# Layer 1's attention written out as a pipeline over three engines, its filler dealt out block by block, one PSUM bank each for values and filler

## The chip, the core and the metric

The kernel runs on one core of a Trainium2 chip. The time is that of one launch on the device, in microseconds (us). Three executions of the kernel before took 1471.29, 1473.4 and 1473.78 us; their median, 1473.4 us, is the time before.

Five engines work in parallel, each through its own list of instructions in a fixed order: PE (matrix products and transposes), DVE and ACT (element by element, reductions, exponentials), POOL (element by element, slower) and SP (starts the transfers). An instruction that has to wait for another engine holds up all that stands behind it on its own engine.

## The reference, cut to what matters

Two layers over 512 latent and 256 context tokens of width 1024. The change is in the attention of layer 1, the last layer, where only the latent tokens are still needed:

```
z = h @ w_in                                     # q (8 heads of 64), k, v (2 heads), u and g of a gated MLP
s = einsum('bkgqd,bkmd->bkgqm', qblk, k)         # per head and 128 queries: 128 x 768 scores
p = softmax(s, axis=-1)
o = einsum('bkgqm,bkmd->bkgqd', p, v)
x = x + ga1 * (concat([attn, gm]) @ w_out)       # gm: the gated MLP's output, ready before the attention
x = x + ga2 * sqrelu_mlp(modulate(rmsnorm(x)))   # 1024 -> 4096 -> 1024
```

Each product is of 32-bit floats. The kernel splits an operand into a high and a low part (two or three products for one); the split is a cast on ACT (`hi`) and a subtraction on DVE or POOL (`lo`).

## The kernel before, in words

Weights come in blocks of 128x1024. SP loads a block into one of two `raw` buffers, ACT casts it to `hi` (L221), POOL or DVE makes `lo` (L222, called a conversion below); five such pairs can be live.

Layer 1's attention has 32 tiles: four pairs of heads j, two blocks of 256 queries, two heads hh, two halves qt of 128 queries. For a tile (`attn_tile`, L1029) PE makes 128x768 scores into one of two `pa` buffers (four matmuls, L217), DVE takes the negated maximum (L1041), ACT the exponential with its sum into a buffer `w` (L1046; tag `w` has three buffers, and L712 takes the same tag for each piece of the q projection, until L733 has read it). In `second`, PE turns the tile by six transposes into two buffers `pt` (L1057), ACT casts them (L1059) and DVE subtracts (L1060). In `third`, once for two tiles (a group), PE makes the values by twelve matmuls into a `pb` buffer (L1080), ACT copies half of it (`pv`, L1087), DVE adds (`mix`, L1088) and, for the second head, multiplies by the softmax factor that PE has transposed next to it (L1084, L1090), and POOL splits the result into Q (L1093, L1094).

Beside that runs the filler: the half of the output projection that works on `gm`, eight outputs m of four k blocks, three matmuls of 128x512 per block (`gm_out`, `proj4`). Each output goes to a `pb` buffer and is added to the residual X by `gate`: in this place ACT scales it (L988) and POOL adds it (L989). The other half, on Q, comes after the attention, by the same `proj4`, with `gate` on DVE (L991). Just ahead of the attention, the last pieces of the q projection are still going through DVE and POOL (L712 to L727), then split (L732, L733) and turned (L745, L746) into Q.

The order on each engine comes from a planner: the program is traced in one sequence, a counter `fl.vt` of estimated time says when deferred steps (`second`, `third`, conversions) and fillers are traced, and a scheduler then puts the instructions of each engine into an order by that sequence and its own cost estimates. In a region under `tc.manual_schedule` an engine's order is that of the trace. `pb` buffers, two in all, were handed out as they came free.

Of the kernel before, what the change touches and what calls it, by code (L numbers as in the profile page):

```python
# [8 lines left out]
F32 = mybir.dt.float32  # L9
# [3 lines left out]
ALU = mybir.AluOpType  # L13
# [19 lines left out]
LATE = (None, None)  # L33


PAR = {"KF": 1, "XO": 1, "MS": 3, "KB": 6, "S0": 200.0, "S2": 1.0, "BK": 1, "CS": 0, "S1": 2400.0, "NS": 2, "CX": 0,
# [135 lines left out]
def trunk(ctx: ExitStack, tc: tile.TileContext, xT, pk1, pk2, rope, wsT, w_mod, w_tok, w_u, w_out, w_ff1, w_ff2, outT):  # L172
# [12 lines left out]
    def nm(s):  # L185
        seq[0] += 1
        return f"{s}_{seq[0]}"
# [7 lines left out]
    def tsm(shape, dt=F32):  # L195
        return tmp.tile(shape, dt, tag="s", name=nm("s"), bufs=3)
# [10 lines left out]
    def pa():  # L207
        return psum.tile([128, 1024], F32, tag="a", name=nm("pa"), bufs=2)

    def pb(shape=(128, 512)):  # L210
        return psum.tile(list(shape), F32, tag="b", name=nm("pb"), bufs=2)

    def pt(shape=(128, 512)):
        return psum.tile(list(shape), F32, tag="t", name=nm("pt"), bufs=2)
# [1 line left out]
    def mm(out, a, b, start, stop, n):  # L216
        pe.matmul(out, a, b, start=start, stop=stop)  # L217
        fl.vt += max(n / 2.4, 113.0) + 3.0

    def split(hi, lo, src, eng=None):  # L220
        act.copy(hi, src)  # L221
        (eng or vec).tensor_tensor(out=lo, in0=src, in1=hi.bitcast(F32), op=ALU.subtract)  # L222
# [5 lines left out]
    ready = []  # L228
    RING = 5

    held = []

    def convert():

# [3 lines left out]
    def pump():  # L238
        while state["live"] < RING and state["pos"] < len(order):
            key = order[state["pos"]]  # L240
            if key == ("ctx",):
                for i in range(4):
                    nc.sync.dma_start(X[i][:, :, SEQ:T], xT[i][:, :, SEQ:T])
                nc.sync.dma_start(k2s[0][:, 128:640], pk2[0][:, 128:640])
                state["pos"] += 1
                continue
            src = dram[key[0]]
            for i in key[1:]:
                src = src[i]
            early = EARLY[state["pos"]] if state["pos"] < len(EARLY) else None  # L250
            if early:
                raw = unit(early, [128, 1024], F32)
            elif key[0] == "mod":

                two = [ring.tile([128, 1024], F32, tag=t, name=nm(t), bufs=RING) for t in ("hi", "lo")]
                for i in range(2):
                    nc.sync.dma_start(two[i], w_mod[0, key[2], key[3] + i])
                ready.append((key, *two))
                state["pos"] += 1
                state["live"] += 1  # L260
                continue
            else:
                raw = ring.tile([128, 1024], F32, tag="raw", name=nm("raw"), bufs=2)
            nc.sync.dma_start(raw, src)
            if key[0] == "mod":
                ready.append((key, raw, None))
                state["pos"] += 1
                continue
            hi = ring.tile([128, 1024], F32R, tag="hi", name=nm("hi"), bufs=RING)
            lo = ring.tile([128, 1024], F32R, tag="lo", name=nm("lo"), bufs=RING)  # L270
            if held is None:
                split(hi, lo, raw, pool_e if "%s%d" % key[:2] in PAR["WP"] else vec)
            else:
                held.append((hi, lo, raw))
            ready.append((key, hi, lo))
            state["pos"] += 1
            state["live"] += 1

    def settle():
        state["live"] -= state["freed"]  # L280
        state["freed"] = 0
        pump()

    def take(*key):
        if not ready:
            settle()
        k, hi, lo = ready.pop([r[0] for r in ready].index(key))
        return hi, lo

# [159 lines left out]
    def region(name):  # L449
        e = PAR["RM"].get(name, "")  # L450
        return tc.manual_schedule(engines={EN[c] for c in e}) if e else nullcontext()
# [235 lines left out]
    def layer(l, h, nxt, K, kv=None, kv0=0):  # L687
# [293 lines left out]
        def gate(i, m, off, n, src):  # L981
            for a, b, cond in ((0, SEQ, 0), (SEQ, T, 1)):
                s, e = max(a, off), min(b, off + n)
                if s < e:
                    xs = xk(m)[:, s:e]
                    if last and i == 2 and done[0] < 8:
                        t = tsm([128, e - s])
                        act.activation(t, src[:, s - off:e - off], AF.Copy, scale=modT[l][:, i * 8 + m, cond:cond + 1])  # L988
                        pool_e.tensor_tensor(out=xs, in0=xs, in1=t, op=ALU.add)  # L989
                        continue  # L990
                    vec.scalar_tensor_tensor(out=xs, in0=src[:, s - off:e - off], scalar=modT[l][:, i * 8 + m, cond:cond + 1], in1=xs, op0=ALU.mult, op1=ALU.add)  # L991

        def proj4(keys, R, i, passes, bank, post=None, gates=None):

            wbs = {}
            for pi, parts in enumerate(passes):
                while gates and not gates[pi]():
                    yield "wait"
                for m in range(8):
                    if m // 2 not in wbs:  # L1000
                        wbs[m // 2] = take(*keys, m // 2)
                    for q, (off, n) in enumerate(parts):
                        if bank == "b":
# [96 lines left out]
        def attention(blks, period):  # L1100
            goal = fl.vt
            for j in range(4):
                for f in turns[0:3 + NP * (1 + j // 2)]:
                    f()
                for blk in blks:
                    st = {}
                    for hh in range(2):
                        for qt in range(2):
                            attn_tile(j, blk, hh, qt, st)
                            fl.tick()  # L1110
                            if last:
                                goal += period
                                fl.fill(goal)
                            else:
                                goal = max(goal, fl.vt) + period
                                fl.step()
                                fl.fill0(goal)

        def gm_out():
            if not GM:  # L1120
                make_gm()
            yield from proj4(("out", l, 0), GM, 2, [dense], "b")
# [36 lines left out]
                    held.append(nr)  # L1159

        fl.fillers = [gm_out(), proj4(("out", l, 1), Q, 2, [[p[0:2]] for p in order2], "b", outpost, gates)]
        with region('att%d' % l):
            if not last:
                fl.fillers = [mods((4, 5)), mixed(fl.fillers[0], mods((6, 7, 8, 9, 10, 11))), fl.fillers[1]]
                attention((2,), PAR["PC"])
            attention((0, 1), PAR["P%d" % l])
        with region('aend%d' % l):
            while done[0] < 8:
                fl.fill(fl.vt + 500.0)
# [233 lines left out]
```

## Time and profile before

| what | value |
|---|---|
| median of three executions | 1473.4 us |
| the profiled execution's own time | 1471.6 us |
| its span | 1469.8 us |
| PE busy | 1437.9 us |
| DVE, ACT, POOL busy | 907.2, 644.2, 379.1 us |
| first scores of layer 1's attention start | 988.35 us |
| first matmul of the output projection on Q starts | 1090.67 us |

All later views are of the profiled execution, in us from the start of its span. A row of the timeline gives start, length, engine, line, operation, output and inputs, and how many equal instructions it merges; in brackets how long the engine had been idle and for whom. On one engine a row's length overlaps the next row's start; from one start to the next is what an instruction takes of its engine.

### The profile page before, as it was taken

To read this page: it belongs to the slowest core of one execution; us is meant where nothing else is said; L and a number is where in the kernel's file an instruction comes from. 1 tells how busy PE (TensorE), PEld (TensorE's weight loads), DVE (VectorE), ACT (ScalarE), POOL (GpSimd) and SP (SyncE) were. 2 spreads that over 40 slices of the span, in tenths; PEclk is the share of its full clock that TensorE was granted. 3 is DMA by queue.
4 is the path that set the end of the run, shared out by engine and by line. 5 is a ranking of instruction groups with operands and counts; after the bars stand their busy time and mean duration, and the time that the engine had idled before them with its cause. 6 is when DMAs were issued, how large, how long until landed. Compare 5 with 4: busy or idle time off the path is not lost.

```text
span 1469.8 us, 21069 instructions
## 1 busy us (share of the span) xinstructions
PE 1437.9 (98%) x8178; PEld 1224.3 (83%) x8178; DVE 907.2 (62%) x1586; ACT 644.2 (44%) x1141; POOL 379.1 (26%) x320
## 2 busy tenths in 40 slices
PE   6999999999999999999999999999999999999998
PEld 3899787988888888888888889997889888888887
DVE  5857867778766564556556547775968554444443
ACT  3552546664545453433325234547855223332221
POOL 0323511222256461323324123277121000000000
PEclk9999999999999999999999999999999999999999
DMA  9322544101233343423343212212002322322331
GB/s 366 116 72 100 188 145 144 59 1 58 90 122 122 118 135 106 136 94 136 106 131 123 88 35 77 96 58 72 16 1 75 120 93 100 100 95 93 100 100 58
DMA packets 50083, 148.71 MB, mean 101 GB/s; under 512 B 5440, under 2 KB 6976, under 8 KB 49984
## 3 DMA queue, kind: packets, MB, share of 16 engines
q1 hardware_dynamic: 49408, 146.72, 29.6%
q8 instruction: 64, 1.05, 0.3%
q10 hardware_dynamic: 576, 0.66, 0.2%
q14 instruction: 35, 0.29, 0.1%
HBM read 145.26 MB, written 2.10 MB: 100 GB/s over the span
## 4 chain that ended last, share of the span: by engine, by line
PE 86%; DVE 7%; ACT 3%; POOL 2%; issue 1%; DMA 1%; SPq 0%; POOLq 0%; ACTq 0%; DVEq 0%
PE pa L217 54%; PE pb L217 23%; PE pt L1057 3%; PE pt L217 2%; PE pb L354 2%; POOL m L298 1%; PE pt L745 1%; DVE lo L222 1%; DMA A<-in_w_mod 1%; POOL lo L222 1%; DVE s L907 0%; ACT hi L221 0%; DVE A L795 0%; ACT w L1046 0%; DVE s L716 0%
## 5 line engine op out<-in xcount | busy, mean ns | idle before, releaser
L217 PE MATMUL pa<-A,hi 128*128 128x512 f32 (+2 forms) x1440 | 429.9, 376 | 0.4 <-ACT A L527 0.2
L221 ACT CAST hi<-raw 128x1024 fp32r<-128x1024 f32 x168 | 176.1, 1049 | 326.9 <-PE pa L217 246.1
L217 PEld LDWEIGHTS pa<-A,hi 128*128 128x128 f32 x1440 | 262.7, 188 | 46.6 <-DVE s L716 0.4
L217 PE MATMUL pa<-A,lo 128*128 128x512 f32 (+2 forms) x832 | 283.8, 347 | 0.0
L222 DVE TENSOR_TENSOR lo<-raw,hi 128x1024 fp32r<-128x1024 f32 x152 | 203.6, 1340 | 122.0 <-ACT hi L221 117.7
L403 POOL TENSOR_TENSOR C<-C,s 128x512 f32<-128x512 f32 x112 | 173.5, 1564 | 296.5 <-ACT s L402 289.8
L217 PE MATMUL pa<-B,hi 128*128 128x512 f32 x750 | 239.0, 391 | 0.0
L217 PEld LDWEIGHTS pa<-A,lo 128*128 128x128 f32 x832 | 156.7, 188 | 21.3
L991 DVE SCALAR_TENSOR_TENSOR X<-pa,modT,X 128x512 f32<-128x512 f32 x168 | 99.8, 614 | 104.6 <-PE pa L217 103.1
L217 PEld LDWEIGHTS pa<-B,hi 128*128 128x128 f32 x750 | 139.9, 188 | 27.2
L217 PE MATMUL pb<-B,hi 128*128 128x512 f32 (+1 forms) x600 | 157.1, 349 | 1.2 <-DVE X L991 1.0
L217 PE MATMUL pa<-B,lo 128*128 128x512 f32 (+1 forms) x450 | 155.2, 354 | 0.0
L217 PE MATMUL pb<-hi,A 128*128 128x256 f32 (+1 forms) x608 | 118.1, 291 | 0.6 <-DVE m L725 0.6
L217 PEld LDWEIGHTS pb<-B,hi 128*128 128x128 f32 x600 | 104.4, 189 | 16.0 <-DVE X L991 2.1
L991 DVE SCALAR_TENSOR_TENSOR X<-pb,modT,X 128x512 f32<-128x512 f32 (+3 forms) x108 | 64.9, 610 | 74.1 <-PE pb L217 74.0
L217 PE MATMUL pb<-B,lo 128*128 128x512 f32 (+1 forms) x300 | 104.1, 347 | 0.0
L217 PEld LDWEIGHTS pb<-hi,A 128*128 128x128 f32 x608 | 96.9, 191 | 2.2 <-PE pb L217 0.8
L217 PEld LDWEIGHTS pa<-B,lo 128*128 128x128 f32 x450 | 84.5, 188 | 14.8
L402 ACT ACTIVATE s<-k,silu 128x512 f32<-128x512 f32 x112 | 77.9, 718 | 35.8 <-DMA k<-in_w_mod 27.8
L217 PE MATMUL pb<-lo,A 128*128 128x256 f32 (+1 forms) x304 | 87.6, 288 | 0.0
L1060 DVE TENSOR_TENSOR A<-pt,A 128x384 fp32r<-128x384 f32 (+1 forms) x144 | 73.6, 536 | 21.1 <-ACT A L1059 19.8
L217 PE MATMUL pb<-A,hi 128*128 128x384 f32 (+2 forms) x288 | 80.4, 360 | 1.1 <-DVE s L833 0.6
(214 smaller groups left out, 2222.6 us busy)
## 6 DMA issues: line engine op xcount, KB each, us to landing
raw<-in_w_ff SPq DMA_DIRECT2D x128, 512.0 KB, 3.5
k<-in_w_mod SPq DMA_DIRECT2D x96, 256.0 KB, 2.8
raw<-in_w_tok SPq DMA_DIRECT2D x16, 512.0 KB, 3.5
raw<-in_w_out SPq DMA_DIRECT2D x16, 512.0 KB, 3.4
lo<-in_w_mod SPq DMA_DIRECT2D x16, 512.0 KB, 4.6
hi<-in_w_mod SPq DMA_DIRECT2D x16, 512.0 KB, 4.0
A<-in_w_mod SPq DMA_DIRECT2D x8, 512.0 KB, 9.8
B<-in_w_mod SPq DMA_DIRECT2D x8, 512.0 KB, 9.6
```

The costliest lines, as they stand in the source:

```text
L217: pe.matmul(out, a, b, start=start, stop=stop)
L221: act.copy(hi, src)
L222: (eng or vec).tensor_tensor(out=lo, in0=src, in1=hi.bitcast(F32), op=ALU.subtract)
L298: pool_e.tensor_tensor(out=y, in0=v, in1=mhalf[:, 0:n], op=ALU.pow)
L354: pe.matmul(ps[q:q + 32, :], S32[:, k, :], ws_[k2 // 2][:, k2 % 2 * 512:(k2 % 2 + 1) * 512], start=k < ns, stop=k >= KT - ns)
L402: act.activation(p, w, AF.Copy, scale=s)
L403: pool_e.tensor_tensor(out=a, in0=a, in1=p, op=ALU.add)
L745: pe.transpose(p[:, o:o + 128], stk[:, t, hh, c0:c0 + 128].bitcast(F32), ident)
L991: vec.scalar_tensor_tensor(out=xs, in0=src[:, s - off:e - off], scalar=modT[l][:, i * 8 + m, cond:cond + 1], in1=xs, op0=ALU.mult, op1=ALU ...
L1057: pe.transpose(tp_[:, (kt - k0) * 128:(kt - k0) * 128 + 128], p[:, kt * 128:kt * 128 + 128], ident)
L1060: vec.tensor_tensor(out=ptl[:, k0:k0 + step, d], in0=src, in1=pth[:, k0:k0 + step, d].bitcast(F32), op=ALU.subtract)
```

## The change

`pipeline()` takes the place of `attention`, `attn_tile` and `gm_out` in layer 1, under a manual schedule for PE, DVE and ACT. It is a loop of 36 steps. Step s traces, in this order: the scores and the maximum of tile s; every fourth step the softmax factors; the turn of tile s-2; half of the twelve value matmuls of a group (tiles s-4 and about it); the exponential of tile s; one k block of the filler (two in step 2, none in steps 11, 12, 21 and 22); in odd steps the mix of a group. Filler blocks left over would follow the loop.

`pb` now has two tags of one buffer each. Where no bank is named, calls take them by turns in the traced order, in both layers. In `pipeline` values take bank 0 and filler bank 1. `gate` loses its way over ACT and POOL: each of the eight filler outputs is added to X by one DVE instruction (L1001 of the changed kernel). Conversions that come up within the loop are put off by `CV` = 6000 of the planner's time, or until the block is taken.

```diff
-    def pb(shape=(128, 512)):
-        return psum.tile(list(shape), F32, tag="b", name=nm("pb"), bufs=2)
+    turn_b = [0]
+
+    def pb(shape=(128, 512), which=None):
+        if which is None:
+            which = turn_b[0]
+            turn_b[0] ^= 1
+        return psum.tile(list(shape), F32, tag=f"b{which}", name=nm("pb"), bufs=1)
...
-            if held is None:
-                split(hi, lo, raw, pool_e if "%s%d" % key[:2] in PAR["WP"] else vec)
+            eng = pool_e if "%s%d" % key[:2] in PAR["WP"] else vec
+            if held is None and state.get("slow"):
+                pend.append((key, hi, lo, raw, eng))
+                fl.defer(PAR["CV"], lambda key=key: settle_one(key))
+            elif held is None:
+                split(hi, lo, raw, eng)
...
-                    if last and i == 2 and done[0] < 8:
-                        t = tsm([128, e - s])
-                        act.activation(t, src[:, s - off:e - off], AF.Copy, scale=modT[l][:, i * 8 + m, cond:cond + 1])
-                        pool_e.tensor_tensor(out=xs, in0=xs, in1=t, op=ALU.add)
-                        continue
                     vec.scalar_tensor_tensor(out=xs, in0=src[:, s - off:e - off], scalar=modT[l][:, i * 8 + m, cond:cond + 1], in1=xs, op0=ALU.mult, op1=ALU.add)
...
+        def out_pieces():
...
+                dst = pb(which=1)
+                for k, (whi, wlo, rhi, rlo) in enumerate(w4(wb, m, GM)):
+                    for i, (a, b) in enumerate(((whi, rhi), (whi, rlo), (wlo, rhi))):
+                        mm(dst, a, b[:, 0:TQ], k == 0 and i == 0, k == 3 and i == 2, TQ)
+                    if k < 3:
+                        yield
+                gate(2, m, 0, TQ, dst)
...
+            for s in range(nt + 4):
+                if s < nt:
+                    if s % 8 == 0:
+                        for f in turns[0:3 + NP * (1 + s // 16)]:
+                            f()
+                    scores(s)
+                if s % 4 == 0 and 0 < s <= nt:
+                    factors(pairs[s // 4 - 1])
+                if 2 <= s < nt + 2:
+                    turned_weights(s - 2)
+                if s >= 4:
+                    values((s - 4) // 2, s % 2)
+                if s < nt:
+                    expo(s)
+                for _ in range(0 if s in (11, 12, 21, 22) else 2 if s in (2,) else 1):
+                    next(pieces, None)
+                if s >= 4 and s % 2:
+                    mixed_heads((s - 4) // 2)
+                fl.tick()
...
+        if last:
+            fl.fillers.pop(0)
+            state["slow"] = True
+            with tc.manual_schedule(engines={mybir.EngineType.PE, mybir.EngineType.DVE, mybir.EngineType.Activation}):
+                pipeline()
+            state["slow"] = False
```

The functions that the loop calls issue the same instructions for a tile as those of the kernel before: scores four matmuls, maximum, exponential, six transposes, two casts, two subtractions, six value matmuls a step.

Where the instructions stand now is seen at three places. The first is PE's list where the attention starts. Of the kernel before, behind the last turn of q (`pt_9670`): `pa_9676` are the scores of tile 0, `pb_9686` the first filler output, whose four k blocks follow each other.

```order
L745 MATMUL pt_9670<-c_70,k_9587 128x128 x4
L217 MATMUL pa_9676<-B_1447_8524,B_1565_9381 128x512
L217 MATMUL pa_9676<-B_1448_8525,B_1565_9381 128x512
L217 MATMUL pa_9676<-B_1447_8524,B_1565_9381 128x256
L217 MATMUL pa_9676<-B_1448_8525,B_1565_9381 128x256
L217 MATMUL pb_9686<-A_1601_9638,hi_9353 128x512 x2
L217 MATMUL pb_9686<-A_1601_9638,lo_9354 128x512
L217 MATMUL pb_9686<-A_1602_9641,hi_9353 128x512 x2
L217 MATMUL pb_9686<-A_1602_9641,lo_9354 128x512
L217 MATMUL pb_9686<-A_1603_9644,hi_9353 128x512 x2
```

Of the change, at the same place: behind the scores of tile 0 (`pa_9678`) one block of the first filler output (`pb_9688`), then the scores of tile 1 (`pa_9692`) and the second block.

```order
L222 MATMUL pa_9678<-B_1448_8525,B_1565_9381 128x256
L222 MATMUL pb_9688<-A_1601_9638,hi_9353 128x512 x2
L222 MATMUL pb_9688<-A_1601_9638,lo_9354 128x512
L222 MATMUL pa_9692<-B_1447_8524,B_1565_9381 128x512
L222 MATMUL pa_9692<-B_1448_8525,B_1565_9381 128x512
L222 MATMUL pa_9692<-B_1447_8524,B_1565_9381 128x256
L222 MATMUL pa_9692<-B_1448_8525,B_1565_9381 128x256
L222 MATMUL pb_9688<-A_1602_9641,hi_9353 128x512 x2
L222 MATMUL pb_9688<-A_1602_9641,lo_9354 128x512
L222 MATMUL pa_9715<-B_1447_8524,B_1565_9381 128x512
```

Eight filler outputs stood in the first eleven tiles; now a block stands in nearly every step. `pb_9688` has bank 1, which the last q projection (`pb_9574`) had drawn by turn just before; its last readers are L712 and L716 on DVE (L727 and L731 of the changed kernel).

The second place is ACT's list at the start of the change: two exponentials (L1171), then the cast of a q piece (L747, L732 before), the casts of tile 0 (L1193), and so on.

```order
L1171 ACTIVATE w_9686,sm_9685<-pa_9678,m_9683 128x768
L1171 ACTIVATE w_9699,sm_9685<-pa_9692,m_9697 128x768
L747 CAST k_9712<-w_9564 128x8x64
L1193 CAST A_1629_9722<-pt_9724 128x3x128
L1193 CAST A_1629_9722<-pt_9730 128x3x128
L1171 ACTIVATE w_9736,sm_9685<-pa_9715,m_9720 128x768
```

And five steps on, behind exponential 4, the last q piece, its two turn copies (L761, L746 before), two weight conversions (L226), and only then the casts of tile 3:

```order
L747 CAST k_9810<-w_9654 128x8x64
L761 CAST B_1590_9558<-pt_9813 128x2x256
L761 CAST B_1591_9559<-pt_9819 128x2x256
L226 CAST hi_9706<-raw_9704 128x1024
L226 CAST hi_9710<-raw_9708 128x1024
L1193 CAST A_1645_9783<-pt_9836 128x3x128
```

In the kernel before, the first of these two q pieces and the two conversions stood ahead of the first exponential or between later ones, where the scheduler had seen room.

The third place is DVE's list at the end of the change: the mix of group 14 (L1221), the last gate of the filler (`pb_10824`), the `lo` of an ff1 weight block (L227), the mix of group 15 (`pb_10889`), the first gate of the projection on Q (`pb_10931`), and the factor of group 15 (L1223).

```order
L1221 TENSOR_TENSOR mix_10882<-pb_10854,pv_10883 64x256
L1001 SCALAR_TENSOR_TENSOR X_4_79<-pb_10824,modT_91,X_4_79 128x512
L227 TENSOR_TENSOR lo_10968<-raw_10965,hi_10967 128x1024
L1221 TENSOR_TENSOR mix_10882<-pb_10889,pv_10908 64x256
L1001 SCALAR_TENSOR_TENSOR X_1_76<-pb_10931,modT_91,X_1_76 128x256
L1223 TENSOR_TENSOR mix_10882<-pb_10889,mix_10882 128x256
```

Before, the filler's gates stood on ACT and POOL and were through by a third of the attention, and that `lo` stood on DVE among the tiles.

More of the change, by code (lines that the diff above doesn't have):

```diff
@@ L33 @@
 LATE = (None, None)
-PAR = {"KF": 1, "XO": 1, "MS": 3, "KB": 6, "S0": 200.0, "S2": 1.0, "BK": 1, "CS": 0, "S1": 2400.0, "NS": 2, "CX": 0,
+PAR = {"KF": 1, "CV": 6000.0, "XO": 1, "MS": 3, "KB": 6, "S0": 200.0, "S2": 1.0, "BK": 1, "CS": 0, "S1": 2400.0, "NS": 2, "CX": 0,
        "FM0": 'DA', "FM1": '', "FC": 7, "MP": [0, 1], "YC": [0, 1], "YK": [0], "RM": {}, "WP": ['out1', 'out0'],
@@ L229, in trunk @@
     RING = 5
-    held = []
+    held, pend = [], []
     def convert():
@@ L282, in settle, with settle_one @@
         pump()
+    def settle_one(key):
+        for e in [e for e in pend if e[0] == key]:
+            pend.remove(e)
+            split(*e[1:])
     def take(*key):
@@ L286, in take @@
             settle()
+        settle_one(key)
         k, hi, lo = ready.pop([r[0] for r in ready].index(key))
@@ L1117, in attention @@
                                 fl.fill0(goal)
+        def out_pieces():
+            if not GM:
+                make_gm()
+            for m in range(8):
+                if m % 2 == 0:
+                    wb = take("out", l, 0, m // 2)
+                dst = pb(which=1)
[5 more added lines that the diff above has]
+                gate(2, m, 0, TQ, dst)
+                if m % 2:
+                    release()
+                yield
@@ new lines, in pipeline, with scores, expo, factors @@
+        def pipeline():
+            tiles = [(j, blk, hh, qt) for j in range(4) for blk in range(2) for hh in range(2) for qt in range(2)]
+            nt, nkt = len(tiles), T // 128
+            pairs, live = [{} for _ in range(nt // 4)], {}
+            pieces = out_pieces()
+            def scores(s):
+                j, blk, hh, qt = tiles[s]
+                qs = slice(blk * 256 + qt * 128, blk * 256 + qt * 128 + 128)
+                ps = pa()
+                for o in range(0, T, 512):
+                    n = min(512, T - o)
+                    for i, kk in enumerate((kA, kB)):
+                        mm(ps[:, o:o + n], Q[j][:, hh, qs], kk[:, j // 2, o:o + n], i == 0, i == 1, n)
+                nmx = small(1)
+                vec.tensor_reduce(out=nmx, in_=ps[:, 0:T], axis=AX.X, op=ALU.max, negate=True)
+                live[s] = ps, nmx
+            def expo(s):
+                ps, nmx = live[s]
+                st = pairs[s // 4]
+                if s % 4 == 0:
+                    st["sm"] = small(4, tag="sm", bufs=3)
+                p = tw([128, T])
+                act.activation(p, ps[:, 0:T], AF.Exp, bias=nmx, accum_out=st["sm"][:, s % 4:s % 4 + 1])
+                live[s] = p
+            def factors(st):
+                rv = small(4, tag="rv", bufs=2)
+                vec.reciprocal(rv, st["sm"])
+                for q in range(2):
+                    st["rc", q] = small(128, tag="rc", bufs=3)
+                    pool_e.tensor_copy(st["rc", q].rearrange("p (h d) -> p h d", h=2), rv.rearrange("p (h q) -> p h q", h=2)[:, :, q:q + 1].broadcast_to([128, 2, 64]))
+            def turned_weights(s):
+                hh, qt = tiles[s][2:]
+                st, p = pairs[s // 4], live.pop(s)
+                if qt == 0:
+                    st[hh] = (unit(f"A{4 + 2 * hh}", [128, nkt, 256]), unit(f"A{5 + 2 * hh}", [128, nkt, 256]))
+                hi, lo = st[hh]
+                d = slice(qt * 128, qt * 128 + 128)
+                for k0 in range(0, nkt, 3):
+                    tp_ = pt()
+                    for kt in range(3):
+                        pe.transpose(tp_[:, kt * 128:kt * 128 + 128], p[:, (k0 + kt) * 128:(k0 + kt) * 128 + 128], ident)
+                    src = tp_[:, 0:384].rearrange("p (a b) -> p a b", b=128)
+                    act.copy(hi[:, k0:k0 + 3, d], src)
+                    vec.tensor_tensor(out=lo[:, k0:k0 + 3, d], in0=src, in1=hi[:, k0:k0 + 3, d].bitcast(F32), op=ALU.subtract)
+                fl.vt += 110.0 * nkt
+            def values(g, half):
+                j, blk, hh, _ = tiles[2 * g]
+                st = pairs[g // 2]
+                if half == 0:
+                    st["o"] = pb(which=0)
+                o = st["o"]
+                for kt in range(3 * half, 3 * half + 3):
+                    for i, s in enumerate(st[hh]):
+                        mm(o[:, 0:256], V[:, kt, j // 2, :], s[:, kt, :], kt == 0 and i == 0, kt == nkt - 1 and i == 1, 256)
+                if half == 0:
+                    return
+                if hh == 0:
+                    st["mix"] = tmp.tile([128, 256], F32, tag="mix", name=nm("mix"), bufs=1)
+                else:
+                    for q in range(2):
+                        pe.transpose(o[:, 256 + q * 128:384 + q * 128], st["rc", q], ident)
+                    fl.vt += 220.0
+                st["pv"] = tmp.tile([64, 256], F32, tag="pv", name=nm("pv"), bufs=1)
+                act.copy(st["pv"], o[64:128, 0:256])
+            def mixed_heads(g):
+                j, blk, hh, _ = tiles[2 * g]
+                st = pairs[g // 2]
+                o, mix = st["o"], st["mix"]
+                vec.tensor_tensor(out=mix[hh * 64:hh * 64 + 64, :], in0=o[0:64, 0:256], in1=st["pv"], op=ALU.add)
+                if hh == 1:
+                    vec.tensor_tensor(out=mix, in0=o[:, 256:512], in1=mix, op=ALU.mult)
+                    b = slice(blk * 256, blk * 256 + 256)
+                    pool_e.tensor_copy(Q[j][:, 0, b], mix)
+                    pool_e.tensor_tensor(out=Q[j][:, 1, b], in0=mix, in1=Q[j][:, 0, b].bitcast(F32), op=ALU.subtract)
+                    done[0] += 1
+            for s in range(nt + 4):
[17 more added lines that the diff above has]
+                fl.tick()
+            for _ in pieces:
+                fl.tick()
@@ L1165, in layer @@
                 attention((2,), PAR["PC"])
-            attention((0, 1), PAR["P%d" % l])
+                attention((0, 1), PAR["P0"])
         with region('aend%d' % l):
```

## The prediction

> **What bounds the kernel now.** I read the page's totals and its chain of waits first, then the busy time by stretches, then the matmuls of the attention in the chain, then the waits at its start.
>
> ```profile
> span 1469.8 us, 21069 instructions
> PE 1437.9 (98%) x8178; PEld 1224.3 (83%) x8178; DVE 907.2 (62%) x1586; ACT 644.2 (44%) x1141; POOL 379.1 (26%) x320
> PE 86%; DVE 7%; ACT 3%; POOL 2%; issue 1%; DMA 1%; SPq 0%; POOLq 0%; ACTq 0%; DVEq 0%
> ```
>
> PE sets the time: 86% of the chain is PE's. Whatever this change can give is idle time of PE. The next view gives stretches (start:end and length, then busy time and instructions of PE, of its weight loads, of DVE, ACT and POOL, then granted clock, DMA share, GB/s).
>
> ```profile
> 240.00:260.00 20.00, 20.00 (x147) 14.98 (x146) 14.86 (x31) 13.35 (x29) 6.95 (x9) 1.00 0.46 159
> ...
> 988.30:1090.60 102.30, 98.69 (x655) 86.17 (x653) 80.11 (x140) 79.18 (x167) 42.20 (x50) 1.00 0.10 32
> 1134.00:1465.00 331.00, 330.92 (x1479) 274.51 (x1479) 158.63 (x187) 95.22 (x122) 0.00 (x0) 1.00 0.29 96
> ```
>
> The stage, from the first scores at 988.35 to the first matmul on Q at 1090.67, is 102.3 us. Behind it PE is full (330.92 of 331), so what the stage gains or loses reaches the end one to one. In layer 0 PE is full too (20.00 of 20).
>
> 98.69 busy does not mean only 3.6 idle: a row's length contains waits inside the pipelined matmul. What PE's work takes is read where the chain of waits stays on PE, each row starting where the one ahead ends.
>
> ```profile
> 1014.11 1.44 PE pb L217 x12
> 1015.55 0.70 PE pa L217 x4
> 1016.26 0.66 PE pt L1057 x6
> 1016.91 2.76 PE pb L217 x12
> ...
> 1025.86 0.22 PE pb L1084 x2
> ```
>
> Values of a group (two tiles) take 1.44, scores 0.70, a turn 0.66, a filler output 2.76 (0.69 for a k block), the turned factors 0.22 per four tiles. A tile is 0.70 + 0.66 + 0.72 + 0.055 = 2.135. The stage's work is 32 x 2.135 = 68.3, filler 8 x 2.76 = 22.1, and four turns of q pieces, 4 x 0.44 = 1.8: 92.2 us.
>
> ```profile
> 1011.40 0.44 PE pt L745 x4
> ```
>
> So **10.1 us of the 102.3 are idle**. Half lies late, when no filler is left. In the chain, the scores that had waited for an exponential stand at
>
> ```profile
> 1061.71 0.50 PE pa L217
> ...
> 1071.29 0.50 PE pa L217
> ```
>
> 9.58 for four tiles, 2.395 for one instead of 2.135. Over the 21 or so tiles from there on without filler: 0.26 x 21 = 5.5. The other 4.6 lie in the first part.
>
> **The change part by part.**
>
> *What every step asks of each engine.* A step with a block is 2.135 + 0.69 = 2.82 of PE. Of DVE and ACT, start to next start:
>
> ```profile
> 1066.34 0.96 DVE L1041 TENSOR_REDUCE m<-pa 128x1 f32<-128x768 f32 x1
> 1067.21 1.01 DVE L1060 TENSOR_TENSOR A<-pt,A 128x384 fp32r<-128x384 f32 x2
> 1068.14 0.41 DVE L1090 TENSOR_TENSOR mix<-pb,mix 128x256 f32<-128x256 f32 x1
> 1068.47 0.17 DVE L1064 RECIPROCAL rv<-sm 128x4 f32<-128x4 f32 x1
> ...
> 1065.28 0.37 ACT L1087 COPY pv<-pb 64x256 f32<-64x256 f32 x1
> 1066.57 0.85 ACT L1059 CAST A<-pt 128x384 fp32r<-128x384 f32 x2
> 1067.39 0.90 ACT L1046 ACTIVATE w<-pa,m 128x768 f32<-128x768 f32 x1
> ```
>
> DVE: 0.87 (1066.34 to 1067.21) + 0.93 (to 1068.14) + three mix instructions in four steps at 0.33, 0.25 + a quarter of a gate. The gate leaves ACT and POOL for DVE; its row is
>
> ```profile
> L991 DVE SCALAR_TENSOR_TENSOR X<-pb,modT,X 128x512 f32<-128x512 f32 (+3 forms) x108 | 64.9, 610 | 74.1 <-PE pb L217 74.0
> ```
>
> 0.61, or 0.15 per step: 2.2 in all. ACT: 0.82 + 1.0 (the chain above has the exponential with its sum's readout at that) + 0.19 = 2.0. Both are under 2.82, so a step with a block is PE's, and the eight gates cost nothing: DVE's 0.6 of slack hides them, and without it they would be 8 x 0.61 = 4.9. The late 5.5 of before go with that, since 32 steps now have work to fill them. Where the waits go:
>
> *Start.* The first block's bank 1 is that of the last q projection, whose last reader is the second of
>
> ```profile
> 992.07 0.74 DVE L716 TENSOR_TENSOR s<-pb,G 128x256 f32<-128x256 f32 x2
> ...
> 988.35 0.94 PE L217 MATMUL pa<-B,B 128*128 128x512 f32 x4
> 989.13 0.62 PE L217 MATMUL pb<-A,hi 128*128 128x512 f32 x2
> ```
>
> that ends at 992.8. Before, the first filler output took the free buffer at 989.13. Now PE stands from 989.05 to 992.9 with the scores of tile 1 queued behind: **3.85**. Then DVE and ACT decide.
>
> ```profile
> 992.73 1.51 DVE L725 TENSOR_SCALAR m<-m 128x8 f32<-128x8 f32 x1
> 971.00 0.16 DVE L725 TENSOR_SCALAR m<-m 128x8 f32<-128x8 f32 x1
> 991.82 2.39 POOL L222 TENSOR_TENSOR lo<-raw,hi 128x1024 fp32r<-128x1024 f32 x1
> 994.15 0.94 DVE L1041 TENSOR_REDUCE m<-pa 128x1 f32<-128x768 f32 x1
> 995.13 0.90 ACT L1046 ACTIVATE w<-pa,m 128x768 f32<-128x768 f32 x1 [2.04 <-DVE m L1041]
> ```
>
> The small L725 took 1.51 and ended at 994.24, just behind POOL's subtraction (994.21); elsewhere it takes 0.16. After the change that subtraction is put off, so the maximum of tile 0 starts at 992.9, its exponential at 993.9, and scores 2 at 995.0; were another POOL operation in its place, 1.2 later. [...]
>
> Tag `w` has three buffers and two hold q pieces, so the exponential after the first waits until turn 0 has read its `w` (before, the second exponential waited likewise for L733):
>
> ```profile
> 1006.32 0.90 ACT L1046 ACTIVATE w<-pa,m 128x768 f32<-128x768 f32 x1 [1.02 <-DVE k L733]
> 991.89 0.62 ACT L732 CAST k<-w 128x512 fp32r<-128x512 f32 x1 [0.39 <-POOL w L727]
> 986.77 0.68 DVE L733 TENSOR_TENSOR k<-w,k 128x512 fp32r<-128x512 f32 x1
> 988.53 1.07 ACT L746 CAST B<-pt 128x512 fp32r<-128x512 f32 x2
> 997.86 1.04 ACT L221 CAST hi<-raw 128x1024 fp32r<-128x1024 f32 x1
> ```
>
> Turn 0 ends at 996.4, exponential 1 at 997.6, then come the q piece's cast and its 0.68 on DVE (998.8), the maximum of tile 2 (999.7) and the subtractions of tile 0 (1000.2 and 1000.65). PE has done the scores of tile 3 by 998.45 and wants turn 1's buffer: **1.8**. In steps 4 to 6 ACT has the last q piece, two copies of 0.5 and two conversions of 1.04 ahead of the casts of tile 3, 0.6 + 1.0 + 2.0 = 3.6 of work against 0.82 of slack (2.82 less 2.0) in each of two steps and 0.1 of lead: **1.85**. Start: 7.5. Bounds: 3.85 alone if the queues absorb the rest, 8.7 with POOL's 1.2.
>
> *Middle.* Steps 11, 12 and 21, 22 have no block (2.135 each) and one conversion of 1.04 sits on ACT behind exponentials 11 and 21. ACT then has 3.0 against 2.135, and its lead is about 0.1: turns 11 and 21 wait some 0.75 each, **1.5**; nothing, if ACT's lead is over 0.9.
>
> *End.* Another conversion behind exponential 31 holds turn 31 by 0.6; values of group 15 wait 0.4 for the mix of group 14 and 0.3 for their subtractions; and the second output on Q needs bank 1 from a gate that stands behind
>
> ```profile
> 1106.03 1.22 DVE lo L222
> ```
>
> and the mix of group 15: 0.75. **2.0**; from 0.4 (the mix alone) to 2.8 (all of the 1.22).
>
> *Layer 0.* `pb` by turns in the traced order moves only a few rows there, and PE is full before. I take 0, with 1 us either way: a block's worth of 0.69, once or twice.
>
> **Sum.** 7.5 + 1.5 + 2.0 = 11.0 idle against 10.1: +0.9. On the profiled execution (span 1469.8, its own time 1471.6, 1.8 around the span) that is 1472.5; the median shown is 1473.4, 1.8 above that execution, so **1474.3 us**.
>
> **The rivals.** *The pipeline holds better than I think (faster).* ACT's and DVE's queues run ahead once the first four steps are through, conversions fall into slack, and there remain 3.85 + 1.8 at the start and 0.4 at the end: 6.05 idle, 4.05 less than before, 1469.4. For it: 2.2 and 2.0 of 2.82 leave each engine 0.6 to 0.8 in 28 steps. Against: the conversions stand right ahead of a cast that PE's next step needs. Its floor is 3.85 alone: 1473.4 - 6.25 = 1467.2.
>
> *One bank each for values and filler closes the loop (slower).* Place: the first value matmul of each group, which waits until mix and, for the second head, the product L1090 have read bank 0. Odd step's mix ends near 3.65 after that step's start, and the next group's first value matmul stands at 2.82 + 0.70 + 0.66 = 4.2 to 4.4: 0.75 of room. It decides from the point where `pv` on ACT, or the DVE work ahead of the mix, is more than 0.75 late; a conversion ahead of `pv` (1.04) is 0.29 too much, one together with the q piece more. Price: 16 groups x 0.35 = 5.6, in place of the 1.5 of the middle: 15.1 idle, +5.0, 1478.4. Against: conversions come at about six places, not sixteen. [...]
>
> *The filler's gate on the path.* Next output's first block could wait for the gate in bank 1: 8 x 0.8 = 6.5 if exposed. Between the last block of an output and the first of the next stand 2.135 of scores, turn and values; the gate is queued behind at most a mix (0.41) and needs 0.61. I count it as hidden; exposed, it is part of the slower case.
>
> *It doesn't do only what it says*: turns in layer 0 cost or save more than the 1 us; in no case I can price from rows does that go beyond.
>
> **How the numbers follow.** This measurement tells changes from none above about 0.2%, 2.9 us. Forecast (stalls exchanged for stalls): 0.46. Faster case: 0.30, since the start's later terms rest on queues that I stacked as late as they can be. Slower case, with the exposed gate: 0.24. The range takes the floor of the faster case and the slower case with 1 us of layer 0: 1467 to 1479.5, leaving out 2 in 10; the forecast alone spans 1471.2 (middle 0, end 0.4) to 1476.3 (start 8.7, end 2.8). Faster 0.30, same 0.46, slower 0.24.
>
> **What would show it.** In the profile after: PE idle from about 989 to 992.9, released by L731 on DVE; turn 1 waiting near 1.8 for the subtraction of tile 0; steps 13 to 20 and 23 to 31 spaced 2.82; turns 11 and 21 late by 0.75, behind L226; around 2 us of gaps at the end; a stage of 103.2 us. It is wrong if steps are spaced over 2.9 and the value matmuls wait for DVE's mix (slower), if the stage is under 100 (faster), or if layer 0's end moves by over 1 us.

## The result and the profile after

The changed kernel takes **1479.9 us** (median of four runs, 1478.56 to 1480.73). The kernel before, run beside it, takes 1472.4 (1471.29 to 1473.78). The ratio is 1.0050, 95% interval 1.0032 to 1.0067: slower by 7.5 us. The forecast was 1474.3, no change; the measured time also lies 0.4 us above the range.

The page of the changed kernel, whose profiled execution took 1480.37 us:

```profile
span 1478.5 us, 21039 instructions
PE 1440.8 (97%) x8178; PEld 1227.3 (83%) x8178; DVE 911.8 (62%) x1594; ACT 638.7 (43%) x1133; POOL 369.5 (25%) x312
PE 86%; DVE 6%; ACT 3%; POOL 2%; issue 1%; DMA 1%; SPq 0%; POOLq 0%; ACTq 0%; DVEq 0%
```

PE has the same 8178 instructions and is 2.9 us longer busy: the work is the same, but part of it ran slower. The view by stretches shows where (PE busy is the second number, the granted clock the third from the right):

```profile
989.90:1096.30 106.40, 98.95 (x643) 87.34 (x641) 81.19 (x144) 72.90 (x157) 29.30 (x40) 0.97 0.08 26
990.84:994.25 3.41, 0.02 (x1) 0.01 (x1) 3.41 (x7) 0.00 (x0) 0.93 (x2) 1.00 0.00 0
994.25:997.66 3.41, 3.38 (x9) 2.84 (x10) 1.26 (x2) 0.99 (x2) 3.33 (x3) 0.50 0.00 0
997.66:1001.07 3.41, 3.41 (x20) 2.85 (x20) 0.51 (x1) 1.48 (x4) 0.54 (x1) 1.00 0.01 2
1001.07:1004.49 3.42, 1.71 (x11) 1.07 (x10) 3.37 (x6) 2.48 (x7) 0.00 (x0) 1.00 0.00 0
1004.49:1007.90 3.41, 3.41 (x12) 2.93 (x13) 2.30 (x4) 1.32 (x4) 0.00 (x0) 0.50 0.00 0
```

PE stood almost all of 990.84 to 994.25, and for the next 3.41 us its clock was 0.50. It was busy for 1.71 of the 3.42 us from 1001.07, and the clock was 0.50 again for 3.41 us. The second stretch shows that PE need not stand throughout one for the next to run at 0.50.

The waits that opened these stretches, in PE's timeline:

```profile
989.92 0.94 PE L222 MATMUL pa<-B,B 128*128 128x512 f32 x4
994.27 1.20 PE L222 MATMUL pb<-A,hi 128*128 128x512 f32 x2 [3.41 <-DVE m L740]
...
1003.21 1.01 PE L1191 MATMUL pt<-c,w 128*128 128x128 f32 x6 [1.60 <-DVE A L1194]
```

These are the two waits that the prediction named: the first filler block for bank 1 (3.85 forecast from the end of the scores; here from 990.6 to 994.27, 3.65), and turn 1 for the subtractions of tile 0 (1.8 forecast, 1.60 measured). The prediction priced each at its own length and did not ask what a PE that stands does to the clock afterwards.

Where the 8.7 us between the two spans (1478.5 and 1469.8) lie:

| part of the span | us |
|---|---|
| up to the first scores (989.92 against 988.35) | +1.6 |
| stage, first scores to first matmul on Q (106.4 against 100.6) | +5.8 |
| behind it | +1.3 |

The 100.6 corrects the prediction, whose stage of before ended too late. PE's timeline of before shows twelve matmuls with an operand `B`, the first output on Q, between the last turned factors and 1090.67:

```profile
1088.83 0.38 PE L1084 MATMUL pb<-c,rc 128*128 128x128 f32 x2
1088.96 0.48 PE L217 MATMUL pb<-B,hi 128*128 128x256 f32 x2
...
1090.67 0.47 PE L217 MATMUL pb<-B,hi 128*128 128x256 f32 x2
```

So the stage of before ended at 1088.96 and had 100.6 - 92.2 = 8.4 us of idle time, not 10.1.

### The profile page after: what moved, and what is told of

Same layout as the page of the kernel before. It is cut to its first block, busy times and chain, and to the rows that moved or that the text cites. A ratio compares the mean times of both kernels' runs of the same rounds, so it can differ in the third digit from the quotient of the medians.

```text
span 1478.5 us, 21039 instructions
## 1 busy us (share of the span) xinstructions
PE 1440.8 (97%) x8178; PEld 1227.3 (83%) x8178; DVE 911.8 (62%) x1594; ACT 638.7 (43%) x1133; POOL 369.5 (25%) x312
## 4 chain that ended last, share of the span: by engine, by line
PE 86%; DVE 6%; ACT 3%; POOL 2%; issue 1%; DMA 1%; SPq 0%; POOLq 0%; ACTq 0%; DVEq 0%
PE pa L222 54%; PE pb L222 23%; PE pb L369 2%; PE pt L222 2%; PE pt L1067 2%; PE pt L1191 1%; POOL m L313 1%; ACT hi L226 1%; PE pt L760 1%; DVE lo L227 1%; DMA A<-in_w_mod 1%; POOL lo L227 1%; DVE s L922 0%; DVE X L1001 0%; DVE A L810 0%
## 5 line engine op out<-in xcount | busy, mean ns | idle before, releaser
L226 ACT CAST hi<-raw 128x1024 fp32r<-128x1024 f32 x168 | 176.0, 1048 | 326.1 <-PE pa L222 243.3
L227 DVE TENSOR_TENSOR lo<-raw,hi 128x1024 fp32r<-128x1024 f32 x152 | 204.6, 1346 | 121.8 <-ACT hi L226 117.4
L1001 DVE SCALAR_TENSOR_TENSOR X<-pa,modT,X 128x512 f32<-128x512 f32 x168 | 99.7, 614 | 104.5 <-PE pa L222 103.0
L1001 DVE SCALAR_TENSOR_TENSOR X<-pb,modT,X 128x512 f32<-128x512 f32 (+3 forms) x116 | 70.7, 619 | 77.5 <-PE pb L222 77.3
L222 PE MATMUL pa<-B,B 128*128 128x256 f32 (+1 forms) x288 | 67.6, 350 | 0.0
```

## The experiments

All were timed in five rounds beside the kernel before. The four of the first set share their runs of it: median 1471.97 of 22. The changed kernel was not timed again with them, and the kernel before took 1472.4 beside it, so a difference to the changed kernel below can be off by about 0.5 us.

### Banks exchanged (swap)

```diff
-                dst = pb(which=1)
+                dst = pb(which=0)
...
-                    st["o"] = pb(which=0)
+                    st["o"] = pb(which=1)
```

> The changed kernel with the two banks exchanged: filler in bank 0, values in bank 1. Bank 0's last user before the loop is an earlier q piece, so the first filler block no longer waits for the last q piece's readers. Theory (the stall at the start, and the half clock that it brings: in the changed kernel the granted clock is 0.50 from 994.25 to 997.66 and again from 1004.5 to 1007.9): the first block follows the first scores at once, PE is idle instead for about 3.3 us ahead of the scores of tile 2 (they wait for exponential 0, that ends near 996.2), the idle time is split over two stretches of 3.41 us, at least one half-clock stretch goes, and the kernel is 1.5 to 3 us faster than the changed one (1477 to 1478.5). Rival (DVE and ACT set the pace at the start, so neither the wait nor the clock is on the path): scores of tile 2 start when they do now, time the same within 0.5 us (1479.5 to 1480.4).

Measured: 1475.54 us, ratio 1.0026 (1.0017 to 1.0035), 4.4 us below the changed kernel (3.9 if each is taken against its own runs of the kernel before), more than the theory's 1.5 to 3. The first wait is gone, and PE stands once, ahead of the scores of tile 2; the halved clock comes later and once, from 996.69 to 1000.10:

```profile
995.18 0.97 PE L222 MATMUL pa<-B,B 128*128 128x512 f32 x4 [3.48 <-ACT w L1171]
...
993.28:996.69 3.41, 1.51 (x11) 1.42 (x12) 1.63 (x2) 0.99 (x2) 3.33 (x3) 1.00 0.00 0
996.69:1000.10 3.41, 3.41 (x11) 2.64 (x10) 1.68 (x3) 2.28 (x6) 0.49 (x1) 0.50 0.01 2
```

The first two rows of the loop's scores are here 1.5 us apart (988.67 and 990.15) instead of 5.8. The wait for the bank was on the path. How much of the 4.4 is the wait and how much the clock, this run alone does not tell.

### PE kept busy, no wait removed (warm)

```diff
+            def warm(n):
+                d = pb(which=0)
+                for _ in range(n):
+                    pe.matmul(d, Q[0][:, 0, 0:128], kA[:, 0, 0:512], start=True, stop=True)
...
+                    if s == 0:
+                        warm(14)
...
+                if s == 3:
+                    warm(6)
```

> The changed kernel with work whose result nobody reads: 14 matmuls of 128x512 (about 3.3 us) into bank 0 behind the scores of tile 0, and 6 (1.4 us) ahead of turn 1, so that PE is busy where it stood. No wait is taken away. Theory (the half clock after the stall costs time of its own): the granted clock stays 1.00 from 990 to 1010, the first block still starts near 994.3, scores of tile 2 come 1.7 us earlier than now, and the kernel is 2 to 3.4 us faster than the changed one (1476.5 to 1478). Rival (slow matmuls lie in the shade of DVE and ACT): clock 1.00 but the time within 0.5 us of the changed kernel, or above it by the added matmuls where they delay the scores behind them (1479.5 to 1481).

Measured: 1476.93 us, ratio 1.0033 (1.0022 to 1.0044), **3.0 us below the changed kernel (2.5 against their own runs of the kernel before) with twenty matmuls more and every wait left in place**. The clock stays at 1.00 in the two stretches that had 0.50:

```profile
994.25:997.66 3.41, 3.41 (x21) 2.98 (x21) 1.52 (x2) 0.99 (x2) 3.33 (x3) 1.00 0.00 0
...
1004.49:1007.90 3.41, 3.35 (x25) 2.88 (x23) 1.69 (x5) 2.42 (x6) 0.53 (x2) 1.00 0.01 2
```

The chain of waits of the changed kernel at the first block, then that of this run at the same place:

```profile
994.27 1.62 PE pb L222 x3
995.90 1.28 PE pa L222 x4
997.18 0.98 PE pb L222 x3
998.15 0.70 PE pa L222 x4
```

```profile
994.02 0.93 PE pb L222 x3
994.95 0.69 PE pa L222 x4
995.64 0.70 PE pb L222 x3
996.34 0.70 PE pa L222 x4
```

The first block still starts where DVE lets it (994.02); scores of tile 2 then follow 2.32 us later instead of 3.88. That is 1.6 for the first stretch. 0.25 us between the two kernels stands already ahead of the first block (994.27 against 994.02). Behind the turn of step 4 they are 3.36 us apart (the chain's next rows start at 1008.22 and 1004.86), 3.1 without that 0.25. The half clock was on the path both times. The rival (slow matmuls in the shade of DVE and ACT) falls.

### The two tags by turns, alone (before_turns)

```diff
-        return psum.tile(list(shape), F32, tag="b", name=nm("pb"), bufs=2)
+        if which is None:
+            which = turn_b[0]
+            turn_b[0] ^= 1
+        return psum.tile(list(shape), F32, tag=f"b{which}", name=nm("pb"), bufs=1)
```

> The kernel before with one part of the change alone: the two pb buffers as two tags of one buffer, taken by turns in traced order, in both layers. The loop, the gates and the conversions are those of before. It tells what the turns cost outside the loop. By the prediction (layer 0 is PE's, 0 within 1 us) and the changed kernel's trace (0.4 us behind at 970): 1472 to 1474 in layer 0's share; in layer 1's attention, where values and filler now draw banks in traced order and not as they come free, up to 3 us more (1473 to 1476). Rival (the turns themselves are what made the changed kernel slower): 1478 to 1481.

Measured: 1471.34 us, ratio 0.9996 (0.9988 to 1.0005). Taking banks by turns in traced order costs nothing, in layer 0 or in the old attention. The prediction's zero for layer 0 holds within its 1 us.

### The filler's gate back on ACT and POOL (gate_old)

```diff
                     xs = xk(m)[:, s:e]
+                    if last and i == 2 and done[0] < 8:
+                        t = tsm([128, e - s])
+                        act.activation(t, src[:, s - off:e - off], AF.Copy, scale=modT[l][:, i * 8 + m, cond:cond + 1])
+                        pool_e.tensor_tensor(out=xs, in0=xs, in1=t, op=ALU.add)
+                        continue
```

> The changed kernel with the gate of the eight filler outputs back on ACT and POOL. By the prediction (DVE's 0.6 us of slack per step hides the gates): the same within 0.7 us (1479.2 to 1480.7); ACT gains 0.7 per output, which can add up to 0.5 per output in steps with a conversion. Rival (the gates on DVE lengthen the steps or the end): 2 us or more faster (under 1478).

Measured: 1480.13 us (five runs), ratio 1.0055 (1.0043 to 1.0068), as the changed kernel. The eight gates on DVE cost nothing that can be measured, as predicted; the interval leaves about 1.8 us either way.

### The filler dealt where PE stood (filled, filled_end)

In the diff, 649 is the planner's time for a block; the line keeps its counter, and with it the places of deferred steps, as in the changed kernel. `filled_end` adds the last two lines.

```diff
-                dst = pb(which=1)
+                dst = pb(which=0 if m == 0 or m >= 2 else 1)
...
-                for _ in range(0 if s in (11, 12, 21, 22) else 2 if s in (2,) else 1):
+                vt = fl.vt
+                for _ in range({0: 1, 1: 6, 2: 5}.get(s, 1 if s < 11 or s % 2 else 0)):
                     next(pieces, None)
+                fl.vt = vt + 649.0 * (0 if s in (11, 12, 21, 22) else 2 if s in (2,) else 1)
...
+                if s < 29:
                     fl.tick()
```

> Banks exchanged as in swap, and the filler dealt where PE stood: 1 block in step 0, 6 in step 1, 5 in step 2 (the second filler output in the other bank, which values need only from step 4), 1 per step up to step 10, then one in every odd step. Theory (the loss is idle PE at the start and the half clock behind it): in swap PE stands 3.5 us ahead of the scores of tile 2 and runs about 3.4 us at half clock; with both filled the clock stays 1.00, the stage gets 4 to 5 us shorter than in swap, and the kernel takes 1469.5 to 1472, level with the kernel before or up to 2 us faster. Rival (a step without a block is paced by DVE and ACT at 2.4 us instead of PE's 2.14, as late in the kernel before): the twelve or so steps that lose their block give back 0.26 us each, 3.1 in all, and it takes 1473 to 1475.

> As filled, and deferred steps (the weight conversions and what else the planner has put off) are not started in the last seven steps of the loop but behind it. Theory (a conversion behind exponential 31 and one ahead of the last mix hold the last turn, the last values and the gate of the first output on Q): 1 to 2 us faster than filled (1468 to 1471). Rival (the conversions then stand in the way of the norm behind the loop, whose work they delay by as much): the same as filled within 0.5 us, or up to 2 us slower.

Measured: 1475.50 us, ratio 1.0019 (1.0010 to 1.0028), and 1474.83, ratio 1.0018 (1.0009 to 1.0027). The figures are near the rival's, but the cause is not its own: the two long waits at the start are gone, the clock is 1.00 from 987 to 1011, and steps without a block take 2.06 to 2.15 us (scores at 1034.33 and 1036.39, 1049.37 and 1051.52). A new wait took the gain. In the chain of `filled`, then ACT's and PE's timelines:

```profile
1009.43 2.40 POOL lo L227
...
1011.85 3.58 DMA raw<-in_w_out
```

```profile
1015.45 1.04 ACT L226 CAST hi<-raw 128x1024 fp32r<-128x1024 f32 x1 [2.99 <-DMA raw<-in_w_out]
```

```profile
1017.51 1.12 PE L760 MATMUL pt<-c,k 128*128 128x128 f32 x8 [3.74 <-DVE A L1194]
```

Filler that runs earlier needs its weights earlier. The next weight block could be loaded only when POOL had finished the `lo` that ended at 1011.83 and so freed a `raw` buffer; the conversion then waited on ACT with the casts of PE's next turn behind it. And the half clock came back: behind this wait the clock of `filled` was 0.50 for one stretch.

```profile
1015.27:1018.68 3.41, 1.17 (x9) 1.11 (x10) 1.68 (x3) 3.17 (x6) 2.11 (x1) 1.00 0.40 144
1018.68:1022.10 3.42, 3.42 (x16) 3.29 (x15) 2.01 (x3) 1.56 (x4) 0.26 (x1) 0.50 0.49 153
```

Leaving the last conversions for behind the loop moved the median by 0.7 us, within the spread of the runs; the 1 to 2 us of its theory did not come.

### Dealt with the weights in view (dealt, dealt2, dealt3)

```diff
-                fl.defer(PAR["CV"], lambda key=key: settle_one(key))
+                fl.defer(PAR["CV"] if key[0] == "out" and key[2] == 0 else 18000.0, lambda key=key: settle_one(key))
...
-                for _ in range({0: 1, 1: 6, 2: 5}.get(s, 1 if s < 11 or s % 2 else 0)):
+                for _ in range({0: 1, 1: 6, 2: 5}.get(s, 1 if 5 <= s <= 33 and (s % 2 or s in (16, 18, 20, 24, 28)) else 0)):
```

> As filled_end, with two causes of filled's own stalls taken away: no block in steps 3 and 4 (in filled the fourth output's first block waited 0.72 us for the gate of the third), and the blocks that follow dealt over steps 5 to 33, one in every odd step and in 16, 18, 20, 24 and 28, so that the third pair of weight blocks is not taken before it can be loaded (in filled a conversion waited 2.99 us for its transfer and PE 3.74 us behind it); conversions of blocks that are not for this filler are put off by three times as long. Theory (the loop itself runs at PE's pace, 2.06 to 2.15 us for a step without a block in filled): the 3.74 and 0.72 go, most of the 0.84 at the end goes too, 4 to 5 us less than filled_end: 1470 to 1471.5, faster than the kernel before by up to 2.5 us. Rival (the waits only move on, since the conversions must be done somewhere on ACT within the stage): 1473 to 1475, no better than filled_end by more than 1.5 us.

Measured: 1472.73 us, ratio 1.0001 (0.9992 to 1.0010): level with the kernel before and 2.1 us below `filled_end`, about half of the expected gain. The 3.74 is gone. In its place turn 2 waits, behind two gates on DVE:

```profile
1003.97 1.01 PE L1191 MATMUL pt<-c,w 128*128 128x128 f32 x6 [1.34 <-DVE A L1194]
```

```profile
1001.18 1.40 DVE L1001 SCALAR_TENSOR_TENSOR X<-pb,modT,X 128x512 f32<-128x512 f32 x2
```

`dealt2` puts those two gates behind the subtractions of tile 1:

```diff
-                gate(2, m, 0, TQ, dst)
+                if m in (1, 2):
+                    later.append((m, dst))
+                else:
+                    gate(2, m, 0, TQ, dst)
...
+                while later and s >= 3:
+                    gate(2, later[0][0], 0, TQ, later[0][1])
+                    later.pop(0)
```

`dealt3` runs the last block in step 31 instead of 33 (the end of the line that deals the blocks):

```diff
-1 if 5 <= s <= 33 and (s % 2 or s in (16, 18, 20, 24, 28)) else 0
+1 if 5 <= s <= 31 and (s % 2 or s in (16, 18, 20, 24, 26, 28)) else 0
```

> As dealt, with one thing moved: on DVE the gates of the second and third filler output stand behind the subtractions of tile 1 (in dealt they stood ahead of the maximum of tile 3, 1.33 us in a row, and turn 2 waited 1.34 us). Theory (each DVE instruction ahead of a subtraction that PE's next turn needs shows in full while PE has no filler left there): 1.0 to 1.4 us faster than dealt, 1471.3 to 1471.8. Rival (the gate then holds the first values, which take its bank): the same as dealt within 0.4 us.

> As dealt2, with the last filler block in step 31 instead of 33, so that its gate is through before the first output on Q needs its bank. Theory (the 0.84 us that the output on Q waits for that gate is exposed): up to 0.8 us faster than dealt2, 1470.5 to 1471.5. Rival (the last steps then have no filler under the latency of the last turns): the same, or up to 0.7 us slower.

Measured: `dealt2` 1472.51 us, ratio 1.0000 (0.9991 to 1.0009): a miss, 0.2 us below `dealt` where 1.0 to 1.4 was expected. The wait of turn 2 is down to 0.16, and one step on PE waits for the same engine:

```profile
1006.16 1.12 PE L760 MATMUL pt<-c,k 128*128 128x128 f32 x8 [1.02 <-DVE A L1199]
```

`dealt3` 1471.65 us against 1472.85 of the kernel before, ratio 0.9991 (0.9982 to 1.0000). The wait for the gate at the first outputs on Q is down from 0.84 to 0.19 and the median 0.9 below that of `dealt2`, as its theory had it. It is 8.3 us below the changed kernel and the lowest of the runs that keep the loop; whether it beats the kernel before, an interval that ends at 1 does not say.

## Why the prediction was wrong

**The step that failed is the pricing of the start.** "Now PE stands from 989.05 to 992.9 ... 3.85" counted the wait and took every later duration at full speed. By the rows of the changed kernel, from the first scores (989.92) to those of tile 8 (1021.27) pass 31.35 us. The work in between is 8 scores, 6 turns, 4 halves of values, 9 blocks, one turn of factors and two q turns at 0.88: 5.6 + 4.0 + 2.9 + 6.2 + 0.2 + 1.8 = 20.7. Idle and slowed time is 10.7, where 7.5 was forecast. The two half-clock stretches together lengthen PE's work by about 3.1 (their chain pieces 1.62 + 1.28 + 0.98 and 1.53 + 1.28 + 1.09 against `warm`'s 0.93 + 0.69 + 0.70 and 0.96 + 0.70 + 0.68). Without them the start is 7.6, near the forecast, and `warm` got 2.5 to 3.0 of it back. That the rest agrees so well is in part luck: the third term, 1.85 for the casts of tile 3, shows only 0.55 and 0.23 of waiting in PE's rows, and about 1.5 lies in short losses around the waits. The mechanism of the bank wait was right; a second one stood behind it. The trace of before had a hint that was not followed: its clock was below 1.00 for one stretch near the start, behind one in which PE was busy for 2.01 of 3.41 us:

```profile
16.15:19.56 3.41, 2.01 (x22) 1.13 (x16) 1.06 (x3) 1.04 (x1) 1.01 (x1) 1.00 1.02 408
19.56:22.98 3.42, 3.02 (x13) 1.06 (x13) 2.38 (x6) 0.72 (x1) 0.00 (x0) 0.50 1.02 408
```

**The end of the stage of before was misread**, which made the idle time to beat 1.7 us too large (10.1 instead of 8.4).

**Other terms.** The middle, 1.5, measured 2.0: from tile 11's scores to tile 14's pass 8.14 us, from 21's to 24's 8.15, for 7.1 of work each. The end within the stage, 2.0 less the 0.75 that lies behind it, measured 1.6 (11.1 us from the scores of tile 31 at 1085.22 to 1096.32, less 9.5 of work). The mechanism behind these is the forecast one; DVE's list at the end reads just as feared, `lo`, mix, then the gate that PE waits for:

```profile
1096.41 1.23 DVE L227 TENSOR_TENSOR lo<-raw,hi 128x1024 fp32r<-128x1024 f32 x1
1097.67 0.42 DVE L1221 TENSOR_TENSOR mix<-pb,pv 64x256 f32<-64x256 f32 x1
1098.12 0.48 DVE L1001 SCALAR_TENSOR_TENSOR X<-pb,modT,X 128x256 f32<-128x256 f32 x1
...
1098.65 0.50 PE L222 MATMUL pb<-B,hi 128*128 128x256 f32 x2 [0.64 <-DVE X L1001]
```

PE's gap there is 0.8 (the last matmul ahead of it starts at 1097.73 and takes 0.12 of PE), and a second of 0.5 follows ahead of 1103.67, 1.3 in all for the forecast 0.75. That is the 1.3 behind the stage. (The exposed gate, 8 x 0.8, is 6.4 and not 6.5; no sum uses it.) The 1.2 for a POOL operation beside the small L725, in the bound of 8.7 alone, was an estimate from one row of before (1.51 us). In the changed kernel the same instruction (L740, at 994.05) took 0.15 with POOL idle until 994.21, so the 1.2 does not show there.

**What held.** Steps with a block are PE's own: in the chain they consist of nothing else, 2.77 each.

```profile
1046.37 0.70 PE pa L222 x4
1047.07 0.65 PE pt L1191 x6
1047.73 1.41 PE pb L222 x9
1049.14 0.70 PE pa L222 x4
```

The gates are hidden (`gate_old`), and so is layer 0 (`before_turns`).

**The rivals.** The slower case had the right sign and a time (1478.4) near the measured one, by a mechanism that did not happen: the first values of a group were to wait for the mix at all 16 groups, an estimate that no run shows. The changed kernel's waits of PE's weight loads (PEld; total, times, longest) name two such:

```profile
PEld pt L1191 <- DVE A L1194: 4.8, 10, 1.8
PEld pb L222 <- DVE mix L1221: 1.0, 2, 0.7
```

By this trace one bank each closes no loop: at most 1.0 us, not the 5.6 of that rival. The faster case left nothing for the middle and 0.4 for the end; 2.0 and 1.6 came there, and the half clock on top. Had the first output drawn the free bank, the change would have cost about 3.6 us (`swap`) instead of 7.5.

**From the forecast to the measured difference**, on the two profiled spans: 0.9 forecast, + 1.7 for the misread end, + 3.2 at the start (3.1 of it half clock), + 0.5 middle, + 0.3 end, + 1.6 ahead of the stage, + 0.6 behind it: 8.8, against 8.7; the rest is rounding.

The 1.6 ahead of the stage was not forecast. 0.4 of it stands since layer 0. The other 1.2 is the meeting of DVE and POOL in the last section; that it is an effect of the change is not shown.

What stays open: the runs do not split the 4.4 us of `swap` into wait, clock and that meeting (DVE's instruction ended first in its profile), and `dealt` regained half of what was expected, the rest being small waits for DVE and ACT that moved when one was taken away.

## What to carry to other kernels

A wait of the matrix engine can cost more than its length, as the 3.4 and 1.6 us here did (about 3.1 us of slowed work behind the two): look at the granted clock in the stretch behind it, and put work there, even useless work, as a test. A fixed bank for a use is only as free as its last user, so ask who read it last ahead of the first use. When filler is moved forward, its weights, their conversions and the buffers they load into have to move with it, and each small wait that is taken away shows the next one.

## What the hardware showed that was not expected

**The clock** kept to stretches of 3.41 us: in the changed kernel it changed at 994.25, 997.66, 1004.49 and 1007.90, one or two such lengths apart, and in the same profile a change at 21.45 lies 972.80 us ahead of that at 994.25, which is 285 times 3.4133. Where these stretches begin differs from execution to execution (996.69 and 1000.10 in `swap`). How much standing is needed, the traces do not settle. `gate_old` has the same second wait of 1.60 us. In its own stretch around it (from 1000.72, which is 241 such lengths behind a half clock at 178.11 of that profile) PE was busy for 1.81 us, and the clock stayed at 1.00 behind it; in the changed kernel 1.71 was followed by 0.50:

```profile
1003.13 1.01 PE L1196 MATMUL pt<-c,w 128*128 128x128 f32 x6 [1.60 <-DVE A L1199]
...
1000.72:1004.13 3.41, 1.81 (x11) 1.13 (x10) 3.08 (x5) 2.48 (x6) 0.00 (x0) 1.00 0.01 2
1004.13:1007.55 3.42, 3.23 (x22) 2.96 (x22) 2.82 (x7) 2.98 (x8) 1.70 (x3) 1.00 0.00 0
```

But the busy time alone does not decide. `filled_end` has the long wait of `filled` (3.67 us, 3.74 there), and the border of two stretches, counted on in that length, falls into the middle of it; with 1.59 and 1.57 us busy in them the clock stayed at 1.00:

```profile
1013.32:1016.73 3.41, 1.59 (x11) 1.11 (x9) 0.73 (x1) 0.50 (x3) 1.98 (x1) 1.00 0.55 186
1016.73:1020.15 3.42, 1.57 (x12) 1.45 (x13) 1.68 (x3) 3.36 (x7) 2.38 (x1) 1.00 0.31 121
1020.15:1023.56 3.41, 3.41 (x28) 3.19 (x27) 2.87 (x6) 2.41 (x6) 0.14 (x1) 1.00 0.41 154
```

So one wait can bring the half clock in one kernel and not in the next (1.60 us in the changed kernel and in `gate_old`, 3.74 in `filled` and 3.67 in `filled_end`). In `gate_old` and `dealt3` a stretch of half clock also stands in layer 0 (from 178.11 and 179.70), where the other nine profiles show 1.00. In the changed kernel a stretch whose longest wait was 1.60 us had the half clock behind it.

**Two instructions that start together.** Just ahead of the stage a DVE subtraction and a POOL addition start at the same moment. In the changed kernel POOL's ended first, after 1.30 us, and DVE's took 1.85; in the kernel before DVE's ended first, after 0.68, and POOL's took 1.82. The changed kernel's rows, then those of the kernel before:

```profile
987.16 1.85 DVE L748 TENSOR_TENSOR k<-w,k 128x512 fp32r<-128x512 f32 x1
987.16 1.30 POOL L732 TENSOR_TENSOR w<-w,s 128x512 f32<-128x512 f32 x1
```

```profile
986.77 0.68 DVE L733 TENSOR_TENSOR k<-w,k 128x512 fp32r<-128x512 f32 x1
986.77 1.82 POOL L717 TENSOR_TENSOR w<-w,s 128x512 f32<-128x512 f32 x1
```

Where POOL's ended first, PE waited 0.92 to 0.96 us ahead of the turn of a q piece. In the eleven profiled executions here POOL's ended first four times (the changed kernel, `warm`, `filled`, `filled_end`) and DVE's seven times (the kernel before, `before_turns`, `swap`, `gate_old` and the three `dealt`). That this is one source of the spread between runs of one kernel is an estimate from that wait; no kernel was profiled several times, so whether chance or the kernel sets the order is not shown.
